# One layer of a hybrid attention and convolution encoder: the embedding's weight in four pieces, its last piece ahead of x, and one sum over partitions queued later

## The chip, the core and the metric

The kernel runs on one core of one Trainium2 chip. The metric is the device time of one execution in microseconds; it is taken three times, and the median is the time of the kernel. A separate execution is recorded by the hardware profiler, and all rows below come from that one. Engines are PE (TensorE, matrix products; PEld is its weight load), DVE (VectorE), ACT (ScalarE), POOL (GpSimd) and SP (SyncE, which here issues nearly all DMAs).

## The reference, cut to what matters

One layer over 1024 positions of width 1024. The input is normalised and projected; four heads of differential attention and four groups of a short gated convolution are made of it; an output projection, a norm and a residual follow. At the end a per-layer embedding `p` is projected, normalised, gated and added:

```python
h = rms_norm(x, pre_norm_gain)
q, k, v, z_a, b_gate, c_gate, u, z_c = jnp.split(h @ w_in, 8, axis=-1)
attn = rms_norm(diff_attention(q, k, v, lam, slopes), subln_gain) * 0.2 * silu(z_a)
conv_out = b_gate * conv3(c_gate * u) * silu(z_c)
x = x + rms_norm(concatenate([attn, conv_out]) @ w_out, post_norm_gain)
e = rms_norm(p @ w_ple_proj, ple_norm_gain)          # p: 1024 x 256
x = x + sigmoid(x @ w_ple_gate) * e
```

## The kernel before

Everything is held transposed: features on the 128 partitions, positions along the row, in two halves of 512 (n = 0 and 1). Each float32 product is made of three matmuls on split operands (`mm3`, L99): the high part times the high part (L100), the high part of the weight times the low part of the data (L101), the low part of the weight times the high part (L102). So each weight is loaded (`raw`), its high part cast by ACT (L89) and its low part subtracted by DVE or POOL (L90) before PE can use it.

The start. `p` (tile `p_raw`, high and low parts `pth`, `pto`) and the embedding's weight (`rawe`, parts `wph`, `wpo`) are loaded first, and `embed(0)` multiplies them, 8 products m = 0 to 7 of six matmuls each (bank `ple`). The weight comes in four pieces for m = 0, m = 1, m = 2 and 3, and m = 4 to 7 (`load_ple`, L300). All four use the pool `rawp`, which has three buffers, so the fourth load waits until the first piece has been read. Then x is loaded (`mix`, `load_x`), scaled by ACT and DVE into `hT`, the operand of all later products (bank `pj`). The results of the embedding are copied to `e` and stored to DRAM (`e_dram`).

The middle. For each head, `PLAN` (L31) lists steps: `a` the softmax of a block of 128 queries (L216: scores on PE into one of three banks `s`, a pass over the bank by DVE with a running minimum, L237, the exponential by ACT, L241, the weighted difference of the two maps by DVE, L249), `v` the load of the values, `g` the product with the values of one half (L252: transposes of the softmax on PE, `tpw`, split into `wt`, matmuls into `av`), `z` and `c` other column blocks of `w_in`. Step `s0` or `s1` (`embed_scale`, L446) reads a half of the stored embedding back, squares it on ACT, adds the eight squares on POOL (L454), and sums over the partitions: a transpose and a reduction on DVE (L107, L109, tile `part`), a matmul with the constant `fold` into `ms` (L116), and a power by POOL (L97) into `rs_e`. `rs_e` is read only in the last stage (L560).

The order on each engine is set by a scheduler when the program is built: it places instructions by its own timeline of the program text, and an engine runs its list strictly in order. `tc.issue_after(i)` asks it to place what is inside no earlier than instruction `i`.

Of the kernel before, what the change touches and what calls it, by code (L numbers as in the profile page):

```python
# [12 lines left out]
F32 = mybir.dt.float32  # L13
F32R = mybir.dt.float32r
# [6 lines left out]
P = 128  # L21
S = 1024
D = 1024
NT = S // P
KT = D // P
# [3 lines left out]
C_PRE, C_CONV, C_SUB, C_POST, C_PLE = 0, 8, 20, 21, 29  # L29
SLOPES = [2.0 ** (-2 * (h + 1)) for h in range(H)]  # L30
PLAN = [  # L31
# [4 lines left out]
]  # L36

# [6 lines left out]
def hybrid_layer(ctx, tc, xT, pT, w_in, lams, w_out, w_ple, w_gate, outT):  # L44
    nc = tc.nc
    V, A, T, G = nc.vector, nc.scalar, nc.tensor, nc.gpsimd
# [5 lines left out]
    wp = ctx.enter_context(tc.tile_pool(name="wp", bufs=3))  # L52
    rawp = ctx.enter_context(tc.tile_pool(name="rawp", bufs=3))
# [12 lines left out]
    def bank_p(name):  # L66
        return ps_s.tile([P, HALF], F32, tag="p", bufs=2, name=name)

    def bank_t(name):
        return ps_s.tile([P, HALF], F32, tag="t", bufs=2, name=name)  # L70
# [16 lines left out]
    def split(hi, lo, src, scale=None, lo_eng=None):  # L87
        if scale is None:
            return (A.copy(out=hi, in_=src),  # L89
                    (lo_eng or V).tensor_tensor(out=lo, in0=src, in1=hi.bitcast(F32), op=sub))  # L90
        else:
            return (A.activation(out=hi, in_=src, func=AF.Copy, scale=scale),
                    V.scalar_tensor_tensor(out=lo, in0=src, scalar=scale, in1=hi.bitcast(F32), op0=mult, op1=sub))

    def rsqrt(out, ssq, n, eps):
        V.tensor_scalar(out=out, in0=ssq, scalar1=1.0 / n, scalar2=eps, op0=mult, op1=add)
        G.tensor_tensor(out=out, in0=out, in1=nhalf[:, :ssq.shape[-1]], op=ALU.pow)  # L97

    def mm3(ps, ah, al, bh, bl, first, last):  # L99
        T.matmul(out=ps, lhsT=ah, rhs=bh, start=first, stop=False)  # L100
        T.matmul(out=ps, lhsT=ah, rhs=bl, start=False, stop=False)  # L101
        T.matmul(out=ps, lhsT=al, rhs=bh, start=False, stop=last)  # L102


    def column_sums(acc, pool, extra=None, tag="flip"):
        flip = pool.tile([P, HALF], F32, tag=tag, name="flip")
        V.transpose(out=flip, in_=acc)  # L107
        part = tiny.tile([P, 32], F32, tag="part", name="part")
        V.tensor_reduce(out=part[:, 0:16], in_=flip.rearrange("p (f r) -> p f r", r=32), axis=AX.X, op=add)  # L109
        if extra is not None:  # L110
            V.tensor_tensor(out=part[:, 16:32].rearrange("p (t f) -> p t f", t=4),
                            in0=extra.unsqueeze(2).broadcast_to([P, 4, 4]),
                            in1=own.unsqueeze(1).broadcast_to([P, 4, 4]), op=mult)
        n = 16 if extra is None else 32
        ms = bank_t("ms")
        T.matmul(out=ms[:, :n], lhsT=fold, rhs=part[:, :n], start=True, stop=True)  # L116
        return ms
# [4 lines left out]
    def load_w(src, pool=None, lo_eng=G):  # L122
# [3 lines left out]
        split(w[:, 0], w[:, 1], raw, lo_eng=lo_eng)  # L126
        return w

    def product(w, rhs, n, bank):
        for kt in range(KT):  # L130
            b = rhs[n][kt]
            mm3(bank, w[:, 0, kt], w[:, 1, kt], b[:, 0], b[:, 1], kt == 0, kt == KT - 1)
        return bank

    def operand(name):
# [8 lines left out]
    def run(tiles, halves=(0, 1), bank=bank_p):  # L144
        for n in halves:
            for w, evac in tiles:
                evac(n, product(w, hT, n, bank("pj")))
# [7 lines left out]
    with ExitStack() as st:  # L155
# [14 lines left out]
        class Head:  # L170
# [81 lines left out]
            def values(s, g):  # L252
                r0 = s.r0
                av = ps_a.tile([P, HALF], F32, tag="a", name="av")
                nj = 4 * g + 4
                for j in range(nj):
                    i0 = max(0, j - 4 * g)
                    tp = bank_t("tpw")
                    for ii in range(i0, 4):
                        T.transpose(out=tp[:, ii * P:(ii + 1) * P], in_=s.ws[ii][:, j * P:(j + 1) * P], identity=ident)  # L260
                    wt = a3.tile([P, 2, HALF], F32R, tag="wt", name="wt")
                    c = slice(i0 * P, HALF)
                    split(wt[:, 0, c], wt[:, 1, c], tp[:, c])
                    mm3(av[:, c], s.vs[:, 0, j], s.vs[:, 1, j], wt[:, 0, c], wt[:, 1, c], j == 0, j == nj - 1)
                sq = ap.tile([P, HALF], F32, tag="sq", name="sq")
                s.last = A.activation(out=sq, in_=av, func=AF.Square)
                o = mix[s.h][g]
                V.tensor_tensor(out=o, in0=av, in1=o, op=mult)
                ms = column_sums(sq, ap, extra=r0)
                rb = tiny.tile([P, 16], F32, tag="rb", name="rb")  # L270
                rs = tiny.tile([P, 16], F32, tag="rs", name="rs")
                V.tensor_copy(out=rb, in_=ms[:, 16:32])
                V.tensor_tensor(out=rs, in0=ms[:, 0:16], in1=rb, op=mult)
                V.tensor_tensor(out=rs, in0=rs, in1=rb, op=mult)
                rsqrt(rs, rs, P, 1e-5)
                V.tensor_tensor(out=rs, in0=rs, in1=rb, op=mult)
                s.rs[g] = rs
# [8 lines left out]
        with ExitStack() as st0:  # L286
# [12 lines left out]

            def load_ple(c, o, queue=nc.sync, constants=0):  # L300
                n = (c.stop - c.start) * 2 * P
                raw = rawp.tile([P, n + constants], F32, tag="raw", name="rawe")
                queue.dma_start(out=raw, in_=w_ple[:, o:o + n + constants])
                if constants:
                    V.tensor_copy(out=sm, in_=raw[:, n:])
                raw = raw[:, :n].rearrange("p (a b c) -> p a b c", b=2, c=P)
                if c.start < 2:
                    V.tensor_copy(out=wph[:, c], in_=raw)
                    V.tensor_tensor(out=wpo[:, c], in0=raw, in1=wph[:, c].bitcast(F32), op=sub)
                else:  # L310
                    split(wph[:, c], wpo[:, c], raw)
# [35 lines left out]
            with tc.issue_after(pt0[2][1].ins):  # L347
                for g in range(4):
                    V.tensor_reduce(out=fold[:, 32 * g:32 * g + 32], in_=ident.rearrange("p (a b) -> p b a", a=4),
                                    axis=AX.X, op=add)  # L350
# [13 lines left out]
        with ExitStack() as st0:  # L364
# [27 lines left out]
            for h in range(H):  # L392
                raw = rawp.tile([P, KT, P], F32, tag="raw", name="raw")
                nc.sync.dma_start(out=raw, in_=w_in[8 + h])
                c = slice(h * P, (h + 1) * P)
                split(wv[:, 0, :, c], wv[:, 1, :, c], raw)
            for j in range(NT):
                c = slice(j % 4 * P, j % 4 * P + P)
                ps = bank_p("v")
                for kt in range(KT):  # L400
                    b = hT[j // 4][kt]
                    mm3(ps, b[:, 0, c], b[:, 1, c], wv[:, 0, kt], wv[:, 1, kt], kt == 0, kt == KT - 1)
                v = v2.tile([P, 2, HALF], F32R, tag="v", name="v")
                split(v[:, 0], v[:, 1], ps, r_col[:, j:j + 1])
                nc.sync.dma_start(out=v_dram[j], in_=v.bitcast(F32))
        ap = st.enter_context(tc.tile_pool(name="ap", bufs=1, reuse_waits="tile"))
# [39 lines left out]
        def embed_scale(n):  # L446

            acc = mix[7][n]
            for m in range(KT):
                e = acc if m == 0 else mix[3 if m % 2 else 6][n]  # L450
                nc.sync.dma_start(out=e, in_=e_dram[n, m])
                A.activation(out=e, in_=e, func=AF.Square)
                if m:
                    G.tensor_tensor(out=acc, in0=acc, in1=e, op=add)  # L454
            r = rs_e[:, 16 * n:16 * n + 16]
            rsqrt(r, column_sums(acc, ap)[:, :16], D, 1e-6)
            V.tensor_scalar(out=r, in0=r, scalar1=0.5, scalar2=None, op0=mult)

        convs = [Conv(ct) for ct in range(4)]
# [10 lines left out]
        for h in range(H):  # L470
            if h > 0:
                hd = Head(h)
                run([(w_in_tile(0, h), hd.ev_q), (w_in_tile(1, h), hd.ev_k)])
            else:
                hd = head0
            for step in PLAN[h]:
                k, v = step[0], step[1:]
                if k == "a":
                    for i in v:
                        hd.softmax(int(i))  # L480
                elif k == "z":
                    run([(w_in_tile(3, h), hd.ev_z)])
                elif k == "v":
                    hd.recall_v()
                elif k == "g":
                    hd.values(int(v))
                elif k == "n":
                    hd.scale_values(int(v))
                elif k == "c":
                    conv_tiles(int(v))  # L490
                elif k == "s":
                    with tc.issue_after(hd.last.ins):
                        embed_scale(int(v))
                elif k == "t":
                    conv_tiles(int(v), together=True)


    with ExitStack() as st:
# [80 lines left out]
        r = post_stat(0)  # L579
# [5 lines left out]
        r = post_stat(1)  # L585
# [46 lines left out]
```

## Time and profile before

| what | us |
|---|---|
| three runs, median (lowest to highest) | 640.5 (640.02 to 640.55) |
| the profiled execution's own time | 640.71 |
| its span, first to last instruction | 638.9 |
| PE busy in the span | 631.2 |
| DVE, ACT, POOL busy in the span | 448.9, 241.7, 227.2 |
| granted TensorE clock, mean of the span | 1.000 |

The profiled execution took 1.8 us more than its span. Busy time of PE counts pipelined matmuls, so a PE that is always busy can still be held up between them: one 512-column matmul lasts 0.39 us, and the next one starts 0.23 us after it. The start times tell that better than the busy share.

### The profile page before, as it was taken

The numbers are of one execution on the slowest core, as the hardware profiler recorded it, in microseconds if no ns is written. First come the engines' busy times: TensorE is split into PE (matmuls) and PEld (weight loads), VectorE is DVE, ScalarE is ACT, GpSimd is POOL, SyncE is SP. The second block draws the span as 40 slices with busy tenths as digits, with TensorE's granted clock in tenths as the row PEclk, the third lists the DMA queues.
The fourth block names the chain that finished last, engine by engine and source line by source line (L and its number), as shares of the span: only waits on it lengthen the run. The fifth ranks groups of instructions, "written<-read, shape, count | busy, mean of one in ns | idle before, by whom it ended". The sixth has DMA issues, their size and how long they took to land.

```text
span 638.9 us, 8065 instructions
## 1 busy us (share of the span) xinstructions
PE 631.2 (99%) x2941; PEld 523.6 (82%) x2941; DVE 448.9 (70%) x825; ACT 241.7 (38%) x441; POOL 227.2 (36%) x114
## 2 busy tenths in 40 slices
PE   8999999999999999999999999999999999999997
PEld 4888888888888888887888888888888888888886
DVE  6978412798786687877886999528992179798342
ACT  5947212433463333542444533223632226313011
POOL 2015100335236545246461142433750087742000
PEclk9999999999999999999999999999999999999999
DMA  8977522310254113342113411100350034124231
GB/s 271 407 285 207 189 98 93 106 34 6 77 153 133 46 34 83 90 144 97 34 42 91 131 34 34 65 35 34 132 230 33 2 98 164 52 83 147 86 113 50
DMA packets 35655, 67.78 MB, mean 106 GB/s; under 512 B 3616, under 2 KB 12448, under 8 KB 35616
## 3 DMA queue, kind: packets, MB, share of 16 engines
q1 hardware_dynamic: 35472, 67.14, 31.9%
q8 instruction: 23, 0.38, 0.2%
q10 hardware_dynamic: 144, 0.13, 0.1%
q14 instruction: 16, 0.13, 0.1%
HBM read 48.38 MB, written 12.58 MB: 95 GB/s over the span
## 4 chain that ended last, share of the span: by engine, by line
PE 92%; DMA 2%; POOL 2%; DVE 1%; ACT 1%; issue 1%; POOLq 0%; ACTq 0%
PE pj L100 15%; PE pj L102 15%; PE pj L101 15%; PE o L102 9%; PE o L100 9%; PE o L101 9%; PE s L233 5%; PE tpw L260 2%; PE v L100 2%; PE v L102 2%; PE v L101 2%; PE av L102 1%; PE av L101 1%; POOL mix L454 1%; PE av L100 1%; PE ple L100 1%
## 5 line engine op out<-in xcount | busy, mean ns | idle before, releaser
L100 PE MATMUL pj<-hT,w 128*128 128x512 f32 x448 | 176.4, 394 | 0.0
L101 PE MATMUL pj<-hT,w 128*128 128x512 f32 x448 | 176.3, 393 | 0.0
L102 PE MATMUL pj<-hT,w 128*128 128x512 f32 x448 | 176.1, 393 | 0.0
L90 POOL TENSOR_TENSOR w<-raw,w 128x1024 fp32r<-128x1024 f32 x41 | 105.7, 2586 | 142.2 <-ACT w L89 142.2
L102 PEld LDWEIGHTS pj<-hT,w 128*128 128x128 f32 x448 | 84.2, 188 | 16.4
L101 PEld LDWEIGHTS pj<-hT,w 128*128 128x128 f32 x448 | 84.2, 188 | 16.2
L100 PEld LDWEIGHTS pj<-hT,w 128*128 128x128 f32 x448 | 84.2, 188 | 16.1
L241 ACT ACTIVATE p<-p,nm 128x128 f32<-128x128 f32 (+7 forms) x64 | 49.4, 773 | 70.4 <-DVE nm L237 60.5
L89 ACT CAST w<-raw 128x1024 fp32r<-128x1024 f32 x44 | 45.8, 1048 | 16.1 <-issue 11.0
L102 PE MATMUL o<-x,w 128*128 128x512 f32 (+1 forms) x136 | 51.3, 377 | 0.0
L100 PE MATMUL o<-x,w 128*128 128x512 f32 (+1 forms) x136 | 51.2, 377 | 0.0
L101 PE MATMUL o<-x,w 128*128 128x512 f32 (+1 forms) x136 | 51.2, 377 | 0.0
L100 PE MATMUL o<-mT,w 128*128 128x512 f32 x128 | 49.8, 389 | 0.0
L101 PE MATMUL o<-mT,w 128*128 128x512 f32 x128 | 49.8, 389 | 0.0
L102 PE MATMUL o<-mT,w 128*128 128x512 f32 x128 | 49.7, 390 | 0.0
L233 PE MATMUL s<-ks,qs 128*128 128x512 f32 (+2 forms) x192 | 47.5, 346 | 0.0
L89 ACT CAST wt<-tpw 128x512 fp32r<-128x512 f32 (+3 forms) x48 | 21.1, 479 | 60.2 <-PE tpw L260 60.2
L90 DVE TENSOR_TENSOR wt<-tpw,wt 128x512 fp32r<-128x512 f32 (+3 forms) x48 | 25.3, 550 | 26.3 <-ACT wt L89 26.1
L237 DVE CUSTOM_DVE_ANT_0 p<-s,bias 128x512 f32<-128x512 f32 (+3 forms) x64 | 34.8, 564 | 9.4 <-PE s L233 5.4
L233 PEld LDWEIGHTS s<-ks,qs 128*128 128x128 f32 x192 | 33.4, 188 | 5.0
L417 POOL TENSOR_TENSOR mix<-mix,R 128x512 f32<-128x512 f32 x8 | 12.3, 1541 | 68.5 <-DVE mix L416 66.4
L249 DVE SCALAR_TENSOR_TENSOR p<-p,rl,p 128x128 f32<-128x128 f32 (+7 forms) x32 | 32.7, 1021 | 0.4
(142 smaller groups left out, 1099.0 us busy)
## 6 DMA issues: line engine op xcount, KB each, us to landing
raw<-in_w_in SPq DMA_DIRECT2D x32, 512.0 KB, 3.8
mix<-in_xT SPq DMA_DIRECT2D x16, 256.0 KB, 5.8
e_dram<-e SPq DMA_DIRECT2D x16, 256.0 KB, 6.0
mix<-e_dram SPq DMA_DIRECT2D x16, 256.0 KB, 3.4
ks<-ks SPq DMA_DIRECT2D x16, 256.0 KB, 3.6
v_dram<-v SPq DMA_DIRECT2D x8, 512.0 KB, 2.6
vs<-v_dram SPq DMA_DIRECT2D x32, 128.0 KB, 2.7
raw<-in_w_out SPq DMA_DIRECT2D x8, 512.0 KB, 3.2
```

Of the source, the lines that this page charges most:

```text
L89: return (A.copy(out=hi, in_=src), (lo_eng or V).tensor_tensor(out=lo, in0=src, in1=hi.bitcast(F32), op=sub))
L90: (lo_eng or V).tensor_tensor(out=lo, in0=src, in1=hi.bitcast(F32), op=sub))
L100: T.matmul(out=ps, lhsT=ah, rhs=bh, start=first, stop=False)
L101: T.matmul(out=ps, lhsT=ah, rhs=bl, start=False, stop=False)
L102: T.matmul(out=ps, lhsT=al, rhs=bh, start=False, stop=last)
L233: T.matmul(out=banks[m][:, :nn], lhsT=s.qs[:, m, qi], rhs=s.ks[:, m, part, c], start=part == 0, stop=part == 1)
L237: V.tensor_tensor_reduce(out=pr[m][:, c0:c0 + n], in0=banks[m][:, :n], in1=s.bias[:, b0:b0 + n], scale=-1.0, scalar=low[m], op0=add, op1=A ...
L241: A.activation(out=pr[m][:, :W], in_=pr[m][:, :W], func=AF.Exp, scale=-1.0, bias=low[m], accum_out=l[:, m:m + 1])
L249: V.scalar_tensor_tensor(out=pr[0][:, :W], in0=pr[1][:, :W], scalar=rl, in1=pr[0][:, :W], op0=mult, op1=add)
L260: T.transpose(out=tp[:, ii * P:(ii + 1) * P], in_=s.ws[ii][:, j * P:(j + 1) * P], identity=ident)
L417: G.tensor_tensor(out=o, in0=o, in1=R[n], op=mult)
L454: G.tensor_tensor(out=acc, in0=acc, in1=e, op=add)
```

## The change

Three things are changed. The weight of the embedding is stored in DRAM piece by piece (one flat array, each piece contiguous), and its fourth piece is loaded into a buffer of the weight pool `wp` instead of `rawp`. `column_sums` can stop at `part`, and the rest of `embed_scale` (the matmul with `fold`, the power and the factor 0.5) becomes a step of its own, `e`, which stands behind the newest matmul of a product or of the values. Step `e0` follows `s0` in head 0; step `e1` stands behind the values `g0` of head 2, where before the sum was made at once in step `s1` of head 1.

```diff
 PLAN = [
-    ['a0123', 'v', 'g0', 'a4567', 'g1', 'c1', 'n0', 'c1', 's0', 'n1', 'c1'],
+    ['a0123', 'v', 'g0', 'a4567', 'g1', 'c1', 'n0', 'c1', 's0', 'e0', 'n1', 'c1'],
     ['a0123', 'z', 'v', 'g0', 'a4567', 'g1', 'c1', 'n0', 'c1', 's1', 'n1', 'c1'],
-    ['a0123', 'z', 'v', 'g0', 'a4567', 'g1', 'c1', 'n0', 'c1', 'n1', 'c1'],
+    ['a0123', 'z', 'v', 'g0', 'e1', 'a4567', 'g1', 'c1', 'n0', 'c1', 'n1', 'c1'],
...
-    def column_sums(acc, pool, extra=None, tag="flip"):
+    def column_sums(acc, pool, extra=None, tag="flip", total=True):
...
-        n = 16 if extra is None else 32
+        return row_sums(part, 16 if extra is None else 32) if total else part
+
+    def row_sums(part, n=16):
         ms = bank_t("ms")
         T.matmul(out=ms[:, :n], lhsT=fold, rhs=part[:, :n], start=True, stop=True)
         return ms
...
-                raw = rawp.tile([P, n + constants], F32, tag="raw", name="rawe")
-                queue.dma_start(out=raw, in_=w_ple[:, o:o + n + constants])
+                if c.start == 4:
+                    raw = wp.tile([P, 2, KT, P], F32R, tag="w", name="w_raw")[:, 0].bitcast(F32).rearrange("p a b -> p (a b)")
+                else:
+                    raw = rawp.tile([P, n + constants], F32, tag="raw", name="rawe")
+                queue.dma_start(out=raw, in_=w_ple[P * o:P * (o + n + constants)].rearrange("(p n) -> p n", p=P))
...
+            return column_sums(acc, ap, total=False)
+
+        def embed_total(n, part):
             r = rs_e[:, 16 * n:16 * n + 16]
-            rsqrt(r, column_sums(acc, ap)[:, :16], D, 1e-6)
+            rsqrt(r, row_sums(part)[:, :16], D, 1e-6)
             V.tensor_scalar(out=r, in0=r, scalar1=0.5, scalar2=None, op0=mult)
...
                     with tc.issue_after(hd.last.ins):
-                        embed_scale(int(v))
+                        part = embed_scale(int(v))
+                elif k == "e":
+                    with tc.issue_after(newest[0].ins):
+                        embed_total(int(v), part)
...
-        "w_ple": c(np.concatenate([ple[:, :1024], small, ple[:, 1024:]], axis=1)),
+        "w_ple": np.concatenate([ple[:, :256].ravel(), ple[:, 256:512].ravel(),
+                                 np.concatenate([ple[:, 512:1024], small], axis=1).ravel(), ple[:, 1024:].ravel()]),
```

`newest[0]` is set to the last matmul by `product` and by `values`.

The list of SP, which issues the loads, begins before the change as follows (`rawe` of width 1024 is the fourth piece, `mix` is x):

```order
L318 DMA p_raw<-in_pT 128x512 x2
L303 DMA rawe<-in_w_ple 128x256
L303 DMA rawe<-in_w_ple 128x549
L297 DMA mix_0_110<-in_xT 128x512
L297 DMA mix_0_112<-in_xT 128x512
L297 DMA mix_0_114<-in_xT 128x512
L303 DMA rawe<-in_w_ple 128x1024
L297 DMA mix_0_116<-in_xT 128x512
```

And it begins after the change as follows (`w_raw` is the fourth piece in its new buffer):

```order
L325 DMA p_raw<-in_pT 128x512 x2
L310 DMA rawe<-in_w_ple 128x256
L310 DMA rawe<-in_w_ple 128x549
L310 DMA w_raw<-in_w_ple 128x1024
L301 DMA mix_0_110<-in_xT 128x512
L301 DMA mix_0_112<-in_xT 128x512
L301 DMA mix_0_114<-in_xT 128x512
L301 DMA mix_0_116<-in_xT 128x512
```

The fourth piece has moved ahead of three loads of x. On PE and DVE its users move with it: ACT casts it before it scales the first three tiles of x, and DVE makes its low part before it scales them.

In the middle the sum's matmul moves on PE, and with it what stood behind it. Before the change PE's list has this piece in a convolution product of the head 1 stage (`pj` with weight `w_2981`; `ms` is the sum of the embedding's second half, `tpw` the transposes for the first values of head 2):

```order
L101 MATMUL pj_3010<-hT1_3_105,w_2981 128x512
L116 MATMUL ms_2265<-part_2263,fold_90 128x16
L260 MATMUL tpw_2641<-ident_85,p0_2493 128x128
L260 MATMUL tpw_2641<-ident_85,p1_2513 128x128
L260 MATMUL tpw_2641<-ident_85,p2_2532 128x128
L260 MATMUL tpw_2641<-ident_85,p3_2551 128x128
L102 MATMUL pj_3010<-hT1_3_105,w_2981 128x512
```

After the change the same sum (now `ms_2692`) stands 51 rows further down, behind the sum that the first values of head 2 need themselves (`ms_2682`):

```order
L101 MATMUL pj_3044<-hT0_0_94,w_3041 128x512
L118 MATMUL ms_2682<-part_2679,fold_90 128x32
L118 MATMUL ms_2692<-part_2263,fold_90 128x16
L102 MATMUL pj_3044<-hT0_0_94,w_3041 128x512
```

And the transposes for those values (now `tpw_2636`) have moved up, to right behind an earlier sum of head 1 (`ms_2109`), one product before (weight `w_2909`):

```order
L101 MATMUL pj_2912<-hT0_2_96,w_2909 128x512
L118 MATMUL ms_2109<-part_2106,fold_90 128x32
L264 MATMUL tpw_2636<-ident_85,p0_2488 128x128
L264 MATMUL tpw_2636<-ident_85,p1_2508 128x128
L264 MATMUL tpw_2636<-ident_85,p2_2527 128x128
L102 MATMUL pj_2912<-hT0_2_96,w_2909 128x512
```

So in that stretch, which held projections alone, PE's list now also holds the transposes and values of head 2's first half and the scores of its second half. One piece of PE's list from there (`s0`, `s1` are score banks, `av` the values) reads:

```order
L237 MATMUL s1_2738<-ks_2336,qs_2335 128x256
L102 MATMUL pj_2944<-hT1_6_108,w_2909 128x512
L237 MATMUL s0_2756<-ks_2336,qs_2335 128x512 x2
L101 MATMUL av_2635<-wt_2651,vs_2626 128x384
L102 MATMUL av_2635<-wt_2651,vs_2626 128x384
L100 MATMUL av_2635<-wt_2660,vs_2626 128x256
L264 MATMUL tpw_2666<-ident_85,p3_2546 128x128
L102 MATMUL pj_2984<-hT0_0_94,w_2981 128x512
L237 MATMUL s1_2757<-ks_2336,qs_2335 128x512 x2
```

On DVE the passes that free those banks move with them, and the pieces of a convolution (`ty`, `mix5`) and of head 1's norm (`rs`) stand between them. Before the change DVE's list at this place reads as follows (`ISA` with `nm` is the pass over a score bank, `flip` the transpose for the embedding's sum):

```order
L237 ISA p1_2700,nm_2697<-s1_2710,bias_2342,nm_2697 128x256
L237 ISA nm_2697 128x1
L439 SCALAR_TENSOR_TENSOR ty_2938<-ty_2938,y_2937 128x512
L276 TENSOR_TENSOR rs_2112<-rs_2112,rb_2111 128x16
L247 RECIPROCAL rl_2720<-l_2698 128x1
L440 SCALAR_TENSOR_TENSOR mix5_0_120<-ty_2938,mix5_0_120 128x512
L436 TENSOR_TENSOR y_2969<-pj_2944,R1_129 128x512
L107 STREAM_TRANSPOSE flip_2261<-mix7_1_125 128x512
```

After the change it reads:

```order
L280 TENSOR_TENSOR rs_2112<-rs_2112,rb_2111 128x16
L241 ISA p1_2727,nm_2725<-s0_2729,bias_2337 128x512
L241 ISA nm_2725 128x1
L253 SCALAR_TENSOR_TENSOR p0_2699<-p1_2700,rl_2720,p0_2699 128x640
L241 ISA p1_2728,nm_2725<-s1_2730,bias_2337 128x512
L241 ISA nm_2725 128x1
L446 SCALAR_TENSOR_TENSOR ty_2938<-ty_2938,y_2937 128x512
L90 TENSOR_TENSOR wt_2651<-tpw_2647,wt_2651 128x384
L447 SCALAR_TENSOR_TENSOR mix5_0_120<-ty_2938,mix5_0_120 128x512
L241 ISA p1_2727,nm_2725<-s0_2737,bias_2337,nm_2725 128x256
```

Five passes over score banks, two parts of the transposes' split and the product with the softmax weight (L253, before L249) now stand ahead of `flip`. The order of POOL's list up to this place, and that of SP's loads in it, is the same as before.

## Rows read from the trace of the kernel before

**Rows 1.** The page's head and its PE row: busy us, share, instructions.

```profile
span 638.9 us, 8065 instructions
PE 631.2 (99%) x2941; PEld 523.6 (82%) x2941; DVE 448.9 (70%) x825; ACT 241.7 (38%) x441; POOL 227.2 (36%) x114
```

**Rows 2.** Waits of PE: who waited for whom, us in total, times, longest.

```profile
PE ple L100 <- ACT wph L89: 0.7, 1, 0.7
PE ms L116 <- DVE part L109: 0.7, 1, 0.7
```

**Rows 3.** The chain that ended last, near the start: start, length, what.

```profile
6.36 5.13 DMA rawe<-in_w_ple
11.51 1.06 ACT wph L89
```

**Rows 4.** Timeline of PE, first 24 us: start, length, engine, line, idle before.

```profile
11.53 0.39 PE L102 MATMUL ple<-pth,wpo 128*128 128x512 f32 x1
12.61 0.50 PE L100 MATMUL ple<-pth,wph 128*128 128x512 f32 x1 [0.69 <-ACT wph L89]
...
22.58 0.39 PE L100 MATMUL pj<-hT,w 128*128 128x512 f32 x1
...
23.94 0.39 PE L101 MATMUL pj<-hT,w 128*128 128x512 f32 x1
```

**Rows 5.** Timeline of SP's issues at the start.

```profile
2.58 1.39 SPq L297 DMA_DIRECT2D mix<-in_xT  x3
```

**Rows 6.** Timelines of ACT and DVE at the start.

```profile
7.10 0.62 ACT L89 CAST wph<-rawe 128x512 fp32r<-128x512 f32 x1 [0.46 <-DMA rawe<-in_w_ple]
...
9.94 0.68 DVE L332 COPY e<-ple 128x512 f32<-128x512 f32 x1
...
13.13 1.22 DVE L90 TENSOR_TENSOR wpo<-rawe,wph 128x1024 fp32r<-128x1024 f32 x1
...
21.19 1.23 DVE L90 TENSOR_TENSOR w<-raw,w 128x1024 fp32r<-128x1024 f32 x1
```

**Rows 7.** Stretches: length, busy PE, PEld, DVE, ACT, POOL, clock, DMA share, GB/s.

```profile
281.00:300.00 19.00, 18.96 (x87) 15.45 (x85) 11.14 (x18) 7.43 (x12) 14.93 (x8) 1.00 0.29 91
300.00:320.00 20.00, 19.36 (x98) 16.41 (x99) 17.68 (x45) 7.79 (x15) 7.37 (x3) 1.00 0.16 53
6.40:9.40 3.00, 3.00 (x14) 2.31 (x14) 2.98 (x10) 1.07 (x3) 0.00 (x0) 1.00 1.01 355
```

**Rows 8.** Timeline of PE around the sum of the second half.

```profile
299.57 0.39 PE L101 MATMUL pj<-hT,w 128*128 128x512 f32 x1
300.64 0.40 PE L116 MATMUL ms<-part,fold 128*128 128x16 f32 x2 [0.69 <-DVE part L109]
```

**Rows 9.** Timeline of POOL in the same stretch.

```profile
288.29 2.91 POOL L97 TENSOR_TENSOR rs<-rs,small_c 128x16 f32<-128x16 f32 x1 [0.32 <-DVE rs L96]
291.17 3.13 POOL L454 TENSOR_TENSOR mix<-mix,mix 128x512 f32<-128x512 f32 x2
295.79 1.30 POOL L454 TENSOR_TENSOR mix<-mix,mix 128x512 f32<-128x512 f32 x1 [1.49 <-ACT mix L452]
297.05 2.40 POOL L90 TENSOR_TENSOR w<-raw,w 128x1024 fp32r<-128x1024 f32 x1
```

**Rows 10.** Timeline of DVE in the same stretch and behind it.

```profile
289.56 0.69 DVE L439 SCALAR_TENSOR_TENSOR ty<-ty,y 128x512 f32<-128x512 f32 x1 [0.36 <-ACT ty L437]
291.24 1.25 DVE L276 TENSOR_TENSOR rs<-rs,rb 128x16 f32<-128x16 f32 x1 [0.98 <-POOL rs L97]
...
297.12 0.71 DVE L107 STREAM_TRANSPOSE flip<-mix 128x512 f32<-128x512 f32 x1 [3.37 <-POOL mix L454]
297.76 2.24 DVE L439 SCALAR_TENSOR_TENSOR ty<-ty,y 128x512 f32<-128x512 f32 x1
...
305.67 0.88 DVE L249 SCALAR_TENSOR_TENSOR p<-p,rl,p 128x640 f32<-128x640 f32 x1
...
309.36 0.67 DVE L237 CUSTOM_DVE_ANT_0 p<-s,bias 128x512 f32<-128x512 f32 x1
```

More of the change, by code (lines that the diff above doesn't have):

```diff
@@ L101, in mm3 @@
         T.matmul(out=ps, lhsT=ah, rhs=bl, start=False, stop=False)
-        T.matmul(out=ps, lhsT=al, rhs=bh, start=False, stop=last)
-    def column_sums(acc, pool, extra=None, tag="flip"):
+        return T.matmul(out=ps, lhsT=al, rhs=bh, start=False, stop=last)
+    def column_sums(acc, pool, extra=None, tag="flip", total=True):
         flip = pool.tile([P, HALF], F32, tag=tag, name="flip")
@@ L127, in load_w @@
         return w
+    newest = [None]
     def product(w, rhs, n, bank):
@@ L131, in product @@
             b = rhs[n][kt]
-            mm3(bank, w[:, 0, kt], w[:, 1, kt], b[:, 0], b[:, 1], kt == 0, kt == KT - 1)
+            newest[0] = mm3(bank, w[:, 0, kt], w[:, 1, kt], b[:, 0], b[:, 1], kt == 0, kt == KT - 1)
         return bank
@@ L263, in values @@
                     split(wt[:, 0, c], wt[:, 1, c], tp[:, c])
-                    mm3(av[:, c], s.vs[:, 0, j], s.vs[:, 1, j], wt[:, 0, c], wt[:, 1, c], j == 0, j == nj - 1)
+                    newest[0] = mm3(av[:, c], s.vs[:, 0, j], s.vs[:, 1, j], wt[:, 0, c], wt[:, 1, c], j == 0, j == nj - 1)
                 sq = ap.tile([P, HALF], F32, tag="sq", name="sq")
```

## The prediction

> **What bounds the kernel now.** I read the page first: PE is busy for 631.2 of 638.9 us [rows 1], so only time in which PE stands still, or starts late, can be won. Next come the waits of PE: apart from the first microseconds they hold two, each of 0.7 us, one in the embedding at the start and one at the sum of its second half [rows 2], and the change is aimed at just these two. The timelines give their full price. The chain of waits says where the first comes from: the load of the weight's fourth piece, issued at 6.36 and landed at 11.49, then ACT's cast of 1.06 [rows 3]. The second is a chain of DVE and POOL [rows 8 to 10].
>
> **The start.** On PE a step is (23.94 - 22.58) / 6 = 0.227 us [rows 4]. Between the starts at 11.53 and 22.58 lie 43 steps, 9.75 us of work in 11.05: 1.30 us are lost, of which the wait at 12.61 holds 0.85 (1.08 less a step) and smaller late starts behind it the rest. The load is late because it needs a buffer that the first piece still fills, and SP, which issues in order, stands still behind it until 6.36, having issued three tiles of x by 3.97 [rows 5]. Now the piece has a buffer of its own and stands ahead of x, so it is issued where those tiles were, near 2.6. It lands behind the third piece, which ACT begins to cast at 7.10 [rows 6], and its 524,288 bytes take 1.48 us at the 355 GB/s of that stretch [rows 7]: about 8.6. ACT casts it in 1.06, to 9.7. DVE makes the low part behind its copy of `e`, which ends at 10.62, in 1.22 [rows 6]: 11.84. PE wants the high part at 11.53 + 0.23 = 11.76 and, by the new list, the low part first at 12.67. Both are there, with 0.8 us in hand at the narrowest. The term is -1.30.
>
> What pays for it is x, whose first three tiles land some 1.4 us later, while the later tiles come sooner, because SP no longer stands still. PE first uses x at 22.58, so the delay is hidden by the 43 products. The narrowest place is DVE's low part of the first weight of `w_in`, at 21.19 for 1.23 [rows 6], which by my count of DVE's new list ends 0.1 to 0.3 us ahead of its use. If that cover is gone, the start returns up to as much as it won: the term lies between -1.30 and 0, and I take -1.30, since only the last 0.1 us of the count is thin. The flat layout and the third buffer of `wp` cost nothing that I can find: the next weight waits for DVE's parts of `p`, long read when it is wanted.
>
> **The sum of the second half.** PE starts at 299.57 and then only at 300.64, 0.84 us more than a step [rows 8]. It waits for `part`. The transpose ahead of that waits 3.37 us for POOL's last addition, and the product `ty` between them takes 2.24 us beside POOL's low part of a weight [rows 9, 10], where the same product took 0.69 at 289.56. The matmul now stands behind the values of head 2, some 51 rows on, when `part` is long there, and the one reader of the result comes in the last stage. The term is -0.84. It could be less only if something else is late at the same spot; that is the next term.
>
> **What moved into its place.** The scheduler has drawn the transposes and values of head 2's first half, and the scores of its second, some 18 us forward into the stretch 281 to 300. There DVE was busy for 11.1 of 19 us, and in the next one 17.7 of 20, at no loss to PE but the wait just told [rows 7]. So DVE has room. But POOL works for 14.9 of those 19 us, and beside it some DVE operations stand still: the product `rs` of 16 columns took 1.25 beside an addition, and `ty` 2.24, whereas `ty` took 0.69 inside POOL's power of 2.91 [rows 9, 10]. Those that stood still read two operands from SBUF and ran beside an addition or a low part. In the new list three such products stand each ahead of a pass that frees a score bank. With POOL's rows 1.30 earlier the additions lie at about 289.9 to 291.2, 291.2 to 293.0 and 294.5 to 295.8, and I go down the list:
> - `rs` (L280) waits for the first addition, and the pass of 0.67 behind it [rows 10] ends at 292.1. PE, counted in its own steps, would reach `s1_2738` at 291.6: 0.5 late.
> - The 640-column product L253 (0.88 alone [rows 10]) waits for the second, and its pass ends at 294.1 for `s0_2756`, due at 293.4 with nothing made up: 0.7.
> - `ty` and `mix5` meet the last one, and the pass for `s1_2757` ends at 297.0 where 296.6 is due: 0.4.
> - The score before these (`s0_2729`) comes 0.25 late by the chain of norm, exponential and split.
>
> That makes 1.9 if nothing is made up. But a bank that is filled late is also read late, so these partly overlap, and I take the three larger without double counting: +1.5. The bounds are 0 (every pass is in time, as in the busier stretch 300 to 320 [rows 7]) and 2.4 (each at its worst).
>
> *A rule beside the trace.* The rows show products of two SBUF operands that last as long as a POOL addition or low part beside them, and one inside a power that does not [rows 9, 10]. The Trainium skill (SBUF — State Buffer, section "SBUF: two separate sides") says that DVE and GpSimd share a port pair as an exclusive lock: an operation with two SBUF inputs waits until a GpSimd operation that came first has ended, and the other way round. The trace agrees for additions (1.25) and low parts (2.24) and not for the power (0.69 inside 2.91). By the rule taken whole the new waits would be an estimated 2.0 us and more; with no lock at all only the 0.25 of the chain would stay. The sum goes by the rows.
>
> **The sum.** -1.30 - 0.84 + 1.5 = -0.64. The profiled execution took 640.71, so 640.07. The median of the runs is 0.21 below it, so the forecast is **639.9 us**.
>
> **The rivals.**
> - *The scheduler's order holds (no new wait).* For it: in the denser stretch behind, PE lost nothing to DVE [rows 7]. Against it: POOL's additions are not there. With 0 to 0.5 of new waits the change gives -2.14 to -1.64: 638.4 to 638.9, so 638.6.
> - *Slower: the end of head 2's softmax is held by POOL.* The added power and what follows it now stand on POOL behind head 2's values. If DVE's product with the softmax weight for the last block waits for a whole power (2.91 [rows 9]), its transposes, due about 317, are late by that. Then +1.5 + 2.9 - 2.14 = +2.3, that is 642.8. It decides as soon as all new waits pass 2.14 + 1.3. Against it: at 289.56 the power did not hold `ty` [rows 10], and PE has projections in its queue there.
> - *The start does not do what it says.* If the queue takes the piece no sooner than x, or the late x costs at 22.58 what was won, the start gives under 0.4: with the middle as forecast, -0.4 - 0.84 + 1.5 = +0.3, that is 640.8. For it: the DMA engines are full from 6.4 to 9.4 [rows 7]. Against it: the piece is asked for before x, and SP's stand-still goes.
>
> **How the numbers follow.** The forecast holds with 0.48, no new wait with 0.36, the slower case with 0.09, the start failing with 0.07. A measurement tells about 0.2%, 1.3 us, from no change: faster is below 639.2, slower above 641.8. The forecast's own range is 639.0 to 641.0, and about a fifth of it is faster. No new wait is faster by nine tenths. So faster is 0.10 + 0.32 = 0.42, less 0.02 for losses outside both stretches: 0.40. Slower is the third case and little of the rest, 0.10; the same is 0.50. The range, 638.2 to 641.5, takes in the second case whole and the fourth, and leaves the slower one out.
>
> **What would show it.** In the profile of the changed kernel: at the start, the fourth piece issued before x and cast near 8.6, no wait of PE for `wph`, and the first product of x near 21.3. At the sum, no wait of `ms` for `part`. Between 285 and 300, waits of PE at score banks (`s`) for DVE's pass, 0.4 to 0.7 each at three places, with L253 or `rs` stretched beside a POOL addition; if there are none, the second case holds. Wrong would be a wait at 21 to 22 for the first weight, or one above 2 us near 317. Since PE has hardly any other idle time, the time should differ from before by just the sum of these.

## The result, and the profile after

The changed kernel takes 646.66 us (median of six runs, 645.28 to 649.2) where the kernel before took 640.51 in the same comparison: a ratio of 1.0099, 95% interval 1.0083 to 1.0114. It is slower by about 6 us, and the forecast was 639.9. The profiled execution took 645.28, 4.57 more than that of before; its span is 643.5.

The page's head and its PE row show that PE does the same work [rows 1]: as many matmuls, 1.1 us more of busy time, 4.6 more of span.

```profile
span 643.5 us, 8059 instructions
PE 632.3 (98%) x2941; PEld 523.5 (81%) x2941; DVE 448.5 (70%) x825; ACT 241.9 (38%) x441; POOL 226.0 (35%) x114
```

The waits of PE (us in total, times, longest) are the shortest way to the loss. Both waits of before [rows 2] are gone, and what was not forecast stands on top:

```profile
PE pj L100 <- DVE mix L451: 3.1, 1, 3.1
...
PE s L237 <- DVE nm L241: 0.8, 2, 0.6
...
PE tpw L264 <- DVE p L253: 0.6, 2, 0.3
```

The timeline of PE says where they are: the end of the embedding, the two score banks, and a product some 140 us behind the last place that the prediction looked at (near 317).

```profile
11.72 0.39 PE L102 MATMUL ple<-pth,wpo 128*128 128x512 f32 x1
11.95 0.40 PE L100 MATMUL ple<-pth,wph 128*128 128x512 f32 x1
...
21.48 0.39 PE L100 MATMUL pj<-hT,w 128*128 128x512 f32 x1
...
294.01 0.73 PE L237 MATMUL s<-ks,qs 128*128 128x512 f32 x2 [0.56 <-DVE nm L241]
...
296.94 0.73 PE L237 MATMUL s<-ks,qs 128*128 128x512 f32 x2 [0.23 <-DVE nm L241]
...
456.78 0.39 PE L102 MATMUL o<-mT,w 128*128 128x512 f32 x1
460.29 0.50 PE L100 MATMUL pj<-hT,w 128*128 128x512 f32 x1 [3.13 <-DVE mix L451]
```

The product at 460.29 belongs to the last convolution tile. It needs a bank of `pj` that DVE's L451 (L444 of the kernel before) must first read. PE was free at 456.78 + 0.23 = 457.01, so 3.28 us are lost.

The account of the profiled execution, where a loss is what lies between two starts on PE beyond a step of 0.227: -1.10 at the start (first product of x at 21.48, before at 22.58 [rows 4]); -0.84 for the sum; +0.73 and +0.48 at the two score banks; +0.48 at 372.6 and +0.45 at 405.7, where transposes wait for the softmax product; +3.28 at 460. That makes +3.48. The other 1.1 of the 4.57 are no single event: from 280 to 320 PE's list now changes more often between long and short matmuls, and starts late by 0.06 to 0.13 us at 22 places, 2.1 us in all, where before there were 11 with 1.0 (a step counted by its columns; the sum's wait and the two banks left out).

**How the late wait comes about.** DVE's timeline of the changed kernel:

```profile
450.01 6.87 DVE L90 TENSOR_TENSOR mT<-mix,mT 128x512 fp32r<-128x512 f32 x4
456.81 2.83 DVE L287 SCALAR_TENSOR_TENSOR mix<-flipa,small_c,mix 128x512 f32<-128x512 f32 x1
459.56 0.68 DVE L451 TENSOR_TENSOR mix<-pj,mix 128x512 f32<-128x512 f32 x1
```

and that of the kernel before, where the same four low parts take 2.49 us and the product with the bank, L444, stands ahead of L283, not behind it:

```profile
447.76 2.49 DVE L90 TENSOR_TENSOR mT<-mix,mT 128x512 fp32r<-128x512 f32 x4
450.17 0.16 DVE L276 TENSOR_TENSOR rs<-rs,rb 128x16 f32<-128x16 f32 x1
450.25 0.68 DVE L444 TENSOR_TENSOR mix<-pj,mix 128x512 f32<-128x512 f32 x1
...
452.65 2.93 DVE L283 SCALAR_TENSOR_TENSOR mix<-flipa,small_c,mix 128x512 f32<-128x512 f32 x1
```

POOL's timelines say why four parts take 2.5 us here and 6.9 there: it makes low parts of three weights of `w_out`, after the change from 450.70, before it from 452.62, when DVE was past the four.

```profile
450.70 8.39 POOL L90 TENSOR_TENSOR w<-raw,w 128x1024 fp32r<-128x1024 f32 x3 [2.64 <-ACT w L89]
```

```profile
452.62 8.04 POOL L90 TENSOR_TENSOR w<-raw,w 128x1024 fp32r<-128x1024 f32 x3 [3.25 <-ACT w L89]
```

And it starts sooner for the same reason: ACT's casts of these weights stood, in the list of before, behind the cast of `mT` that needs L444's result; with L451 late they stand ahead of it. The three waiting products (two of the four, 2.90 and 2.88, and L287) each last as long as one of POOL's low parts (2.79 to 2.83). So a new order on DVE and ACT, 160 us away from the moved sum, costs more than the edit's own places.

### The profile page after: what moved, and what is told of

It is laid out like the page before. It is cut to its first block, busy times and chain, and to the rows that moved or that the text cites. A ratio compares the mean times of both kernels' runs of the same rounds, so it can differ in the third digit from the quotient of the medians.

```text
span 643.5 us, 8059 instructions
## 1 busy us (share of the span) xinstructions
PE 632.3 (98%) x2941; PEld 523.5 (81%) x2941; DVE 448.5 (70%) x825; ACT 241.9 (38%) x441; POOL 226.0 (35%) x114
## 4 chain that ended last, share of the span: by engine, by line
PE 76%; DVE 12%; issue 5%; POOL 4%; ACT 2%; DMA 1%; ACTq 0%; DVEq 0%; POOLq 0%
PE pj L100 10%; PE pj L101 10%; PE pj L102 10%; PE o L102 9%; PE o L100 9%; PE o L101 9%; PE s L237 3%; PE v L100 2%; PE v L102 2%; PE v L101 2%; DVE p L253 2%; DVE p L241 2%; PE tpw L264 2%; POOL w L90 1%; POOL rs L97 1%
## 5 line engine op out<-in xcount | busy, mean ns | idle before, releaser
L424 POOL TENSOR_TENSOR mix<-mix,R 128x512 f32<-128x512 f32 x8 | 10.8, 1349 | 67.2 <-DVE mix L423 65.1
L253 DVE SCALAR_TENSOR_TENSOR p<-p,rl,p 128x128 f32<-128x128 f32 (+7 forms) x32 | 32.7, 1022 | 0.3
```

Source lines behind the costliest of these rows:

```text
L253: V.scalar_tensor_tensor(out=pr[0][:, :W], in0=pr[1][:, :W], scalar=rl, in1=pr[0][:, :W], op0=mult, op1=add)
L424: G.tensor_tensor(out=o, in0=o, in1=R[n], op=mult)
```

## The experiments

In the diffs below `...` marks lines left out, and the comments are added.

**The parts alone.** `start_only` is the changed kernel without the step `e`:

```diff
...
-            return column_sums(acc, ap, total=False)
-
-        def embed_total(n, part):
             r = rs_e[:, 16 * n:16 * n + 16]
-            rsqrt(r, row_sums(part)[:, :16], D, 1e-6)
+            rsqrt(r, column_sums(acc, ap)[:, :16], D, 1e-6)
...
```

> Only the start is changed (flat weight, fourth piece in a buffer of the weight pool ahead of x); the sum of the second half stays in step s1. Theory: the late wait of 3.1 us at 460 comes from the moved sum alone, because DVE's list here has the convolution's product (L451) ahead of flipa and L287, as before the change. Then the start gives what it gave in the changed kernel, about -1.1 to -1.3: 639.2 to 639.5, ratio 0.998, and no wait of PE above 0.4 us after 320. Rival: the late wait comes from everything lying 1.1 us earlier, so that POOL's low parts meet DVE in another phase: then 641 to 643 with a wait near 450 to 460.

Measured: 639.54 against 640.46, ratio 0.999 (0.9981 to 0.9999). Apart from PE's first wait for its zeros, its waits are only the sum's and one of 0.2 at the start:

```profile
PE ms L118 <- DVE part L109: 0.7, 1, 0.7
PE ple L100 <- ACT pth L89: 0.2, 1, 0.2
```

This trace cannot settle the rival, for its execution, at the upper end of the eleven (641.02; the shortest took 639.09), does not lie earlier. Until 10.1 us PE's products start every 0.42 to 0.43 us, where a step is 0.227, and the first product of x comes at 22.89, later than before the change:

```profile
9.27 0.63 PE L100 MATMUL ple<-pth,wph 128*128 128x512 f32 x1
9.69 0.63 PE L101 MATMUL ple<-pto,wph 128*128 128x512 f32 x1
...
22.89 0.39 PE L100 MATMUL pj<-hT,w 128*128 128x512 f32 x1
```

The six other traces with the new start have that product at 21.00 to 21.48, where the kernel before has 22.58 and `bad_order_before`, which keeps the old start, 22.43: the start itself is worth 0.95 to 1.58 us. The rival falls by two other runs: `sum_only` has the late wait without the new start, and `part_first` (below) lies earlier, with that product at 21.12, keeps the sum in its place and has no late wait. `sum_only` is the other half:

```diff
-                if c.start == 4:
-                    raw = wp.tile([P, 2, KT, P], F32R, tag="w", name="w_raw")[:, 0].bitcast(F32).rearrange("p a b -> p (a b)")
-                else:
-                    raw = rawp.tile([P, n + constants], F32, tag="raw", name="rawe")
-                queue.dma_start(out=raw, in_=w_ple[P * o:P * (o + n + constants)].rearrange("(p n) -> p n", p=P))
+                raw = rawp.tile([P, n + constants], F32, tag="raw", name="rawe")
+                queue.dma_start(out=raw, in_=w_ple[:, o:o + n + constants])
...
```

> Only the sum over partitions is moved; the start is that of the kernel before. Theory: all the loss is here. The wait of ms goes (-0.84), score banks cost 1.9 between 280 and 320, about 0.9 at the product with the softmax weight near 373 and 406, and the bank freed by L448 about 3.3 near 461: about 645 to 646 at full clock, ratio 1.008 to 1.010. Rival, that both parts are needed for the late wait: 641 to 642.

Measured: 648.56, ratio 1.0124 (1.011 to 1.0138). All the loss is in the moved sum, and the same waits stand in its profile (3.12 at 461.60, 0.55 and 0.28 at score banks). It is 3 us more than expected, and its trace shows what comes on top. The granted clock falls to half within the long wait and stays there until about 467.6 (stretches, as in [rows 7]; the last three columns are clock, DMA share, GB/s):

```profile
461.60:464.00 2.40, 2.40 (x6) 1.92 (x7) 2.24 (x4) 1.73 (x3) 0.00 (x0) 0.50 1.02 386
464.00:466.00 2.00, 2.00 (x6) 1.55 (x5) 1.97 (x4) 1.44 (x2) 0.00 (x0) 0.50 0.93 364
466.00:468.00 2.00, 2.00 (x7) 1.57 (x6) 1.44 (x2) 1.26 (x3) 1.80 (x1) 0.59 0.34 128
468.00:472.00 4.00, 4.00 (x19) 3.31 (x18) 4.00 (x6) 3.13 (x5) 2.11 (x2) 1.00 0.59 188
```

**The late wait.** `product_first` puts L451 ahead of L287 again. Its lists are otherwise those of the changed kernel, but for this place: PE's product, too, stands five matmuls further up, and a few instructions of DVE and ACT shift:

```diff
-    [..., 'n0', 'c1', 'n1', 'c3', 't2'],
+    [..., 'n0', 'c1', 'c3', 't2', 'n1'],
...
-                V.tensor_tensor(out=o, in0=ps, in1=o, op=mult)
+                s.b = getattr(s, "b", []) + [V.tensor_tensor(out=o, in0=ps, in1=o, op=mult)]
...
+                elif k == "n" and h == H - 1 and v == "1":
+                    with tc.issue_after(convs[3].b[0].ins):   # L451, first half
+                        hd.scale_values(1)
```

> The changed kernel with head 3's last factor (flipa, L287, second half) placed behind the convolution's product L451 on DVE, as the list of the kernel before has it. Theory: the 3.1 us at 460 are DVE's order there, L451 standing behind a product that meets a POOL low part of a weight; with L451 one pair earlier it ends near 454 to 457 and the wait goes: 3 us off the changed kernel, 642 at full clock. Rival, POOL's three low parts starting 1.1 us earlier than before hold DVE whatever the order of these two: less than 1 us off, 644 to 645.

Measured: 641.71, ratio 1.0023 (1.0013 to 1.0033), and no wait near 460. Its timelines of DVE and POOL:

```profile
448.80 2.49 DVE L90 TENSOR_TENSOR mT<-mix,mT 128x512 fp32r<-128x512 f32 x4
451.21 0.68 DVE L451 TENSOR_TENSOR mix<-pj,mix 128x512 f32<-128x512 f32 x1
```

```profile
453.58 10.87 POOL L90 TENSOR_TENSOR w<-raw,w 128x1024 fp32r<-128x1024 f32 x4 [6.10 <-ACT w L89]
```

Both things of before are back: L451 early, and POOL's low parts behind it, since ACT's casts wait for it. `low_parts_later` separates the two. It keeps the lists of PE, DVE and ACT and makes POOL wait, by one small product more in POOL's own list:

```diff
+                if s.ct == 3 and n == 0:
+                    d = tiny.tile([P, 16], F32, tag="rs", name="rsd")
+                    s.g = G.tensor_tensor(out=d, in0=o[:, :16], in1=o[:, :16], op=mult)
...
+            A.copy(out=w[:, 0], in_=raw)
+            with tc.issue_after(behind):      # s.g, for three weights of w_out
+                G.tensor_tensor(out=w[:, 1], in0=raw, in1=w[:, 0].bitcast(F32), op=sub)
...
```

> The changed kernel, its DVE list kept, with POOL's low parts of three weights of w_out waiting for the convolution's product L451 (a POOL product of 16 columns that reads its result stands ahead of them). Theory of the shared port: the four mT products and L287, 6.9 and 2.8 us in the changed kernel, then take 2.5 and 0.75, L451 is done near 454, and PE's wait of 3.1 us goes: 642 at full clock. Rival, they are long because of late operands (ACT's casts) or of the order alone: they stay long and the time stays within 0.5 us of the changed kernel's 645.3.

Measured: 642.22, ratio 1.0037 (1.0023 to 1.005). The same six DVE instructions, in the same order, with POOL's low parts now behind them (its first starts after the 16-column product at 453.54):

```profile
449.74 2.46 DVE L90 TENSOR_TENSOR mT<-mix,mT 128x512 fp32r<-128x512 f32 x4
452.12 0.75 DVE L292 SCALAR_TENSOR_TENSOR mix<-flipa,small_c,mix 128x512 f32<-128x512 f32 x1
452.78 0.69 DVE L456 TENSOR_TENSOR mix<-pj,mix 128x512 f32<-128x512 f32 x1
```

6.87 became 2.46 and 2.83 became 0.75: the products were long because POOL's low parts stood beside them, and the wait of 3.28 comes of it. `bad_order_before` was to be the other half of that question, the order without POOL's meeting:

```diff
-                V.scalar_tensor_tensor(out=o, in0=flip, scalar=subg, in1=o, op0=mult, op1=mult)
+                s.scaled = V.scalar_tensor_tensor(out=o, in0=flip, scalar=subg, in1=o, op0=mult, op1=mult)
...
-                V.tensor_tensor(out=o, in0=ps, in1=o, op=mult)
+                with tc.issue_after(hd.scaled.ins) if (s.ct, n) == (3, 0) else nullcontext():
+                    V.tensor_tensor(out=o, in0=ps, in1=o, op=mult)
```

> The kernel before, with one thing changed: on DVE the last convolution's product for the first half (its L444, here L445) stands behind head 3's last factor (L283), as in the changed kernel. If that order alone makes the late wait, PE waits about 3 us near 460 and the time is 643.5 or more. If it also needs DVE's four low parts mT to fall beside POOL's low parts, as they do in the changed kernel (from 450.0, POOL from 450.7) and not here (from 447.8), PE waits under 1 us and the time is 640.5 to 641.5. I hold the second for likelier.

Measured: 640.39, ratio 0.9996 (0.9987 to 1.0005), no wait near 460. But a meeting is there, a smaller one. Timelines of DVE, POOL and PE:

```profile
447.40 2.48 DVE L90 TENSOR_TENSOR mT<-mix,mT 128x512 fp32r<-128x512 f32 x4
449.81 2.37 DVE L276 TENSOR_TENSOR rs<-rs,rb 128x16 f32<-128x16 f32 x1
...
453.43 2.14 DVE L283 SCALAR_TENSOR_TENSOR mix<-flipa,small_c,mix 128x512 f32<-128x512 f32 x1
455.50 0.68 DVE L445 TENSOR_TENSOR mix<-pj,mix 128x512 f32<-128x512 f32 x1
```

```profile
449.25 8.60 POOL L90 TENSOR_TENSOR w<-raw,w 128x1024 fp32r<-128x1024 f32 x3 [0.25 <-ACT w L89]
```

```profile
456.47 0.39 PE L100 MATMUL pj<-hT,w 128*128 128x512 f32 x1
```

With L445 late, POOL's low parts start at 449.25 where the kernel before has 452.62: the order alone brings them forward, as told above. They hold two DVE products here, L276 (2.37) and L283 (2.14), since the four low parts are done by then. L445 is done at 456.18, 5.3 us later than L444 was and 0.3 us ahead of PE's product, which the scheduler put ten matmuls further down its list. So this run does not try the order without the meeting, and "in time" is narrow. What it shows is that the order with two held products is not enough. In the changed kernel three are held, for DVE reaches the four at 450.01 and not at 447.40: there L280 and `flipa`, which wait for POOL's power, stand ahead of them. That last step is read from the rows, not tried alone; that without any meeting there is no wait is shown by `low_parts_later`.

**The score banks.** `no_additions` is `product_first` without POOL's additions of that half, so the sum is that of its first tile only:

```diff
...
-                if m:
+                if m and n == 0:
                     G.tensor_tensor(out=acc, in0=acc, in1=e, op=add)
...
```

> As product_first, but POOL's seven additions of the embedding's second half are left out, so the sum of that half is that of its first tile only. The scheduler then orders the stretch anew, so the rows tell more than the time. Theory: the two waits of PE at score banks, 0.57 and 0.22 us, come from DVE products standing still beside additions; without them L253 of 640 columns takes 0.9 and not 1.34, L447 0.7 and not 1.46, and no score bank is waited for near 293 and 296: about 1 us off product_first. Rival, the passes are too dense there in any case: the waits stay within 0.2 us of what they were.

Measured: 639.53, ratio 0.999 (0.998 to 1.0); no score bank is waited for. In the changed kernel DVE took longer for the products with two operands from SBUF:

```profile
291.93 1.42 DVE L253 SCALAR_TENSOR_TENSOR p<-p,rl,p 128x640 f32<-128x640 f32 x1
...
294.95 1.53 DVE L447 SCALAR_TENSOR_TENSOR mix<-ty,mix 128x512 f32<-128x512 f32 x1
```

beside these additions of POOL:

```profile
289.99 2.68 POOL L461 TENSOR_TENSOR mix<-mix,mix 128x512 f32<-128x512 f32 x2
294.64 1.30 POOL L461 TENSOR_TENSOR mix<-mix,mix 128x512 f32<-128x512 f32 x1 [1.97 <-ACT mix L459]
```

and without them the same two take their own time:

```profile
289.89 0.69 DVE L447 SCALAR_TENSOR_TENSOR mix<-ty,mix 128x512 f32<-128x512 f32 x1
...
294.04 0.88 DVE L253 SCALAR_TENSOR_TENSOR p<-p,rl,p 128x640 f32<-128x640 f32 x1
```

L252, of a single column and just ahead, has 0.73 in the changed kernel and 0.21 here. So the rows bear out that the additions stretch these products, by 0.5 to 0.8 us each. That the banks came in time for this reason alone they do not show, since the stretch was ordered anew and L253 now stands behind the pass that it had held up; nor does the time, 2.2 us below `product_first`, twice what was expected.

**The sum without the move.** `part_first` is `start_only` with one DVE instruction held back:

```diff
...
-                V.scalar_tensor_tensor(out=t, in0=t, scalar=1.0, in1=y, op0=add, op1=mult)
+                with tc.issue_after(hold[0].ins) if (s.ct, n) == (1, 1) else nullcontext():  # the reduction to part
+                    V.scalar_tensor_tensor(out=t, in0=t, scalar=1.0, in1=y, op0=add, op1=mult)
...
```

> As start_only, and the sum of the second half stays where the kernel before has it, but on DVE the reduction that it waits for stands ahead of the convolution's product ty, which there takes 2.2 us beside a POOL low part. Theory: the reduction is then ready near 298.6 and the wait of 0.84 goes without drawing anything forward: 638.4 to 638.9, ratio 0.997 to 0.998. Rival, another reader of DVE becomes late in its place: 639.3 to 640.

Measured: 638.82 against 640.65, ratio 0.9977 (0.9968 to 0.9986), the best version here, 1.8 us below the kernel before. The reduction that waited behind `ty` [rows 10] is done at 297.29, and PE passes `ms` without a stop:

```profile
296.60 0.69 DVE L111 TENSOR_REDUCE part<-flip 128x16 f32<-128x512 f32 x1
```

```profile
297.65 0.39 PE L102 MATMUL pj<-hT,w 128*128 128x512 f32 x1
297.88 0.29 PE L120 MATMUL ms<-part,fold 128*128 128x16 f32 x2
298.02 0.64 PE L266 MATMUL tpw<-ident,p 128*128 128x128 f32 x4
```

Here, too, the scheduler changed the lists of PE and DVE behind the edit, at some forty places; the one new wait is 0.2 us at a score bank (308.06). None of it became a late wait.

**The clock.** `changed_again` is the changed kernel, unedited.

> The changed kernel once more, beside the others on one chip. The three microseconds that PE waits near 460 were followed by the half clock in sum_only, for 14 matmuls at 0.43 us and not 0.23, 2.8 us. If the wait brings that on, runs of this kernel fall into two groups, near 645.3 with a mean clock of 1.0 and near 647 to 648 with 0.993 to 0.997, and product_first, without the wait, has no such second group at a lower clock. Rival, the chip's own variation: the lower clock shows in runs of the kernel before as often.

Measured: 646.23 to 647.0 in four runs, ratio 1.0097 (1.0083 to 1.0111), mean clock 0.997 in all four. The eleven runs of `product_first` have 0.998 to 1.000, and of the 21 and the 27 runs of the kernel before two and one had 0.997. With `sum_only`, 12 of the 14 runs of kernels with the wait have 0.993 to 0.997; of the 58 runs of the edited kernels without it none has. The trace of `changed_again`, in the stretch up to the wait's end and the two behind it:

```profile
455.00:459.90 4.90, 1.80 (x8) 1.14 (x7) 4.90 (x4) 0.00 (x0) 3.73 (x2) 0.94 0.90 317
459.90:462.00 2.10, 2.07 (x5) 1.69 (x6) 1.94 (x4) 1.45 (x3) 0.00 (x0) 0.50 0.85 295
462.00:466.00 4.00, 4.00 (x18) 3.23 (x17) 3.40 (x5) 3.41 (x7) 1.45 (x1) 0.91 0.85 328
```

The two groups are there, but not evenly: among the ten runs of the two comparisons two were at 1.0 (645.28 and 645.45), the others at 0.993 to 0.997. So the wait of 3.1 us costs twice, once as itself and then, in most runs, as half a clock (1.2 of 2.4 GHz) for a few microseconds behind it. Three runs of `product_first` near 643.5 have a clock of 0.999 to 1.0, so this does not explain them. The slow steps of PE until 10.1 us in `start_only`'s trace show one thing that makes an execution longer by 1.4 to 1.9 us (first product of x at 22.89, not at 21.00 to 21.48); no trace of those three runs was kept to tell whether it was that.

## Why the prediction was wrong, step by step

The start was right. The piece was to be cast from 8.6 and its low part to be there at 11.84; the timelines of ACT and DVE have

```profile
8.31 1.05 ACT L89 CAST wph<-w_raw 128x1024 fp32r<-128x1024 f32 x1 [0.73 <-DMA w_raw<-in_w_ple]
```

```profile
10.73 1.21 DVE L90 TENSOR_TENSOR wpo<-w_raw,wph 128x1024 fp32r<-128x1024 f32 x1
```

and PE went from 11.72 to 21.48 in steps, without a stop: 9.76 us for the 43 steps, where 9.75 was said. The term came to -1.10 in this execution, where -1.30 was said, because PE reached the first of these steps at 11.72 and not at 11.53. The six traces named above have the first product of x at 21.00 to 21.48, around the 21.3 of the forecast. The time of `start_only` alone (639.54 for 640.46, ratio 0.999) is at the edge of what can be told.

The sum's own wait went, as said, -0.84.

The new waits at score banks were placed rightly and summed a little high. `s0_2756` was to be 0.7 late and was 0.73; `s1_2757` was to be 0.4 late and was 0.48; `s1_2738`, to be 0.5 late, was 0.1 late (292.06), because `rs` took 0.16 between two additions; L252 ahead of it had waited out the first. That is 1.21 where 1.5 was taken. The cause is the one given as far as the products' lengths go (L253 1.42 for 0.88, L447 1.53 for 0.69). The many small late starts, 1.1 us more than before, were in no term.

The step that failed is the last one: that the time differs from before by just the sum of the terms named, so that outside both stretches nothing changes; for losses there the prediction kept 0.02 of chance, and gave no row or list for it. It reads the lists of DVE only in the stretch of the sum. They differ down to the end of the attention, and those of ACT with them, since the scheduler orders by its own timeline and everything behind the moved values shifts in it. Of +4.57, 3.28 come from one place of that new order and 0.93 from two more, at which the softmax product L253 meets a low part of POOL (2.95 us at 369.62, 3.38 at 402.30; read from the rows, not tried alone). The median lies 1.4 us above the profiled 645.28; four of the six runs have a lower clock, 0.993 to 0.997, which fits what `changed_again` shows, though none of the four was traced. The slower rival was right in one thing, that POOL holds DVE and PE then waits about 3 us, which passes the gain; that its 2.9 is near the 3.28 is luck, for it named POOL's power and the end of head 2's softmax, near 317, where no wait came. What held DVE were the low parts of `w_out`, near 455, and it was the bank of a convolution that was late.

What drew the values forward can be read from the lists, and has not been run: the sum's bank and the banks of the transposes come from one pool of two buffers, handed out in the order of the text. Where the sum stands ahead of head 2's values, even one step ahead (`e1` behind `z`), all lists come out as in `start_only`. So by the lists the sum had held the values back, and its wait of 0.84 came with an order that was otherwise good. And the products that fill the stretch, of which the section on the change speaks as head 1's, are by their numbers those of head 2's first convolution steps.

*The rule beside the trace, once more.* The rows show two-operand products standing still beside POOL's low parts (6.87 for four, 2.46 without) and additions (1.42 for 640 columns, 0.88 without). The Trainium skill (SBUF — State Buffer, section "SBUF: two separate sides") has this as an exclusive lock of a port pair, held for the whole instruction, and the trace agrees for these. With POOL's power it still does not: in the row at 289.56 [rows 10] a product of 0.69 ran inside one.

## What to carry to other kernels

Where a scheduler sets the order, compare the order of every engine to the end of the program, and look above all at reads of PE's banks that have moved behind other work; a gain of a microsecond at the edit is smaller than one such place. Where PE waits for an engine, first take away what stands ahead of the awaited instruction (here one reduction set ahead of one product: 638.82 where `start_only` has 639.54) before its consumer is moved. And list what DVE does with two operands from SBUF beside POOL's long instructions: here such a product lasted up to a whole POOL instruction, 2.83 to 2.90 us beside low parts of 2.79 to 2.83, where it takes 0.65 to 0.75 without them.

## What was not expected of the hardware

In two of the three traces with the wait of 3.1 us the granted clock fell to 0.50 within it and stayed there for the first 2.8 us (`changed_again`) or 6.0 us (`sum_only`) of the matmuls behind it; in the third it was 1.00 throughout. In `sum_only` matmuls then started every 0.43 us, some fourteen of them, where a step is 0.23: 2.8 us more, nearly the wait again.
